# Triangles of all eight chunks issued together on four quarters of TensorE's array

## The chip, the cores and the metric

One core of a Trainium2 chip runs one program. TensorE (PE) multiplies matrices and writes to PSUM, of which it has eight banks; VectorE (DVE), ScalarE (ACT) and GpSimd (POOL) do elementwise work; transfers are issued from SyncE's queue (SP). The metric is the device time of one execution in microseconds. Three executions of the kernel before took 1361.43, 1364.46 and 1368.26 us.

## The reference

One layer over 256 latent tokens and 256 context tokens, each 2048 wide: a modulated norm, one wide input projection, two branches (RWKV-7 with 16 heads of 64, gated linear attention with 4 heads), two projections back, an output projection and a last norm. What matters here is the RWKV branch's scan, in both directions (`d`), context first, then latent:

```
def step(s, inp):
    w_t, k_t, v_t, a_t, b_t = inp[:5]
    sa = jnp.einsum("bhvk,bhk->bhv", s, a_t)
    s = s * w_t[:, :, None, :] + sa[..., None] * b_t[:, :, None, :] + v_t[..., None] * k_t[:, :, None, :]
    y = jnp.einsum("bhvk,bhk->bhv", s, inp[5]) if emit else None
```

## The kernel before

The scan is done in eight chunks of 64 tokens for each direction: four of context (`g` = 0) and four of latent tokens (`g` = 1). The 16 heads go in eight pairs `p`; a pair's two heads `hd` lie in the two halves of the 128 partitions. For each chunk the products of `a` and `b` inside it make a strictly triangular 64 x 64 matrix (a "triangle"), and the chunk's step needs the inverse of one minus it. The path of a pair:

- `fe_track` makes the factors `ar` (with decays, for `a` and `r`) and `bk` (for `b` and `k`).
- `ab_track` multiplies them to the triangles: 16 matmuls of 64 x 64 x 64 in fp32 for the context chunks into one PSUM bank (`pab`), an eviction with a mask into `AB` on DVE, and the same once more for the latent chunks. Head 0 uses the upper left quarter of the array (rows and columns 0 to 63), head 1 the lower right one.
- `gg_track` makes the value products, of which those of the first four chunks are `pgc`: 16 matmuls, with head 0 and head 1 in two row halves, both written to the same output half (`vs`), so into two banks.
- `inv_track` copies parts of `AB` to `Lin` and `GMo` (ACT), transposes `Lin` to `M` (DVE), and inverts the 32 x 32 triangles with 60 instructions on POOL (`tm`, `M`). Two transposes (`Lin<-M`), small matmuls (`pH`, `pZ`) and copies make the inverse `Z`.
- `sc_track` then runs the eight steps of the scan: `p1`, `R`, `pU`, `UV`, `pSs`, `Sn` and the output `pY`, on PE, ACT and DVE in turn.

All eight pairs' tracks are interleaved by a planner (`Issue`) when the program is built: it keeps a clock for each engine from rough costs, and issues the work that can start first, by priority. Between the small matmuls it places the dense stream (`acc`), the projections, whose weights are split into two parts `wH` (ACT) and `wL` (DVE) and multiplied three times. Each engine then runs its list in order. `pab`, `pgc` and the other small products share three banks (`g3`), claimed by the planner.

Of the kernel before, what the change touches and what calls it, by code (L numbers as in the profile page):

```python
# [12 lines left out]
OP = mybir.AluOpType  # L13
# [4 lines left out]
P = 128  # L18
# [58 lines left out]
class Issue:  # L77
# [136 lines left out]
    def rel(self, x):  # L214
        nm = x.tensor.name
        b = self.bank_of.pop(nm)
        self.busy.discard(b)
        self.bank_free[b] = self.rd.get(nm, 0.0)
# [112 lines left out]
def hybrid_layer(tc, a, out):  # L331
    nc = tc.nc
    es = ExitStack()
    with es:
# [6 lines left out]
        iss = Issue(ps, {"acc": (0, 1, 2, 3), "pa": (4, 5, 6, 7), "gg": (4, 5, 6, 7), "st": (2,), "u1": (3,), "py": (4,),  # L341
                         "g3": (5, 6, 7), "o2": (2, 3),
                         "f4": (0, 1, 2, 3, 4, 5, 6), "s1": (7,), "s2": (6, 7),
                         "xp": (0, 1, 2, 3, 4, 5, 6, 7)})
        rel = iss.rel
        engs = (nc.vector, "dve"), (nc.scalar, "act"), (nc.gpsimd, "pool"), (nc.tensor, "pe"), (nc.sync, "dma")
        V, S, G, T, Q = (Eng(iss, e, k, False) for e, k in engs)
        DV, AC, PO, PE, DM = (Eng(iss, e, k, True) for e, k in engs)
# [610 lines left out]
        def chunk(i, d):  # L959
            return i if d == 0 else (3 - i if i < 4 else 11 - i)  # L960
# [9 lines left out]
        def half(hd):  # L970
            return slice(64 * hd, 64 * hd + 64)
# [5 lines left out]
        RW = {}  # L977
# [127 lines left out]
        def ab_track(p, xp):  # L1105

            yield lambda: ("feat", p) in DONE and (p == 0 or ("lin", p - 1) in DONE)
            ar, bks = RW[p]["ar"], RW[p]["bks"]
            AB = RW["AB"]
            xb = p % 2  # L1110
            for g in range(2):
                pa = yield Claim("g3", [P, 4, 2, 64], "pab", *bks, ar)
                yield [PE.matmul(pa[half(hd), i, d, :], bks[d][half(hd), chunk(4 * g + i, d), xb, :], ar[half(hd), d, i, g, :],
                                 start=True, stop=True) for i in range(4) for d in range(2) for hd in range(2)]
                yield DV.tensor_tensor(AB[:, 4 * g:4 * g + 4], pa, RW["m_t"][:, None, None, :].to_broadcast([P, 4, 2, 64]), op=OP.mult)
                rel(pa)
            DONE.add(("ab", p))

        def gg_track(p, fp, xp):

            yield lambda: ("ab", p) in DONE
            s = RW[p]
            ar, bks = s["ar"], s["bks"]
            GM, GMr, BK = s["GM"], s["GMr"], s["BK"] = tuple(RW[n][p % 2] for n in ("GM", "GMr", "BK"))
            vs = rows(p)[1]
            xk = 1 - p % 2
            left = [6]

            def done():
                left[0] -= 1  # L1130
                if not left[0]:
                    DONE.add(("gg", p))

            def mask(m, n, r):
                return m[r, p % 2, None].to_broadcast([r.stop - r.start, n, 2, 64])

            def ev_c(pg, hd):
                yield DV.tensor_tensor(GM[vs, hd, 0:4], pg[vs], mask(m_ab, 4, vs), op=OP.mult)
                rel(pg)
                done()  # L1140

            def ev_l(pg, hd, i):
                yield DV.tensor_tensor(GM[vs, hd, 4 + i:6 + i], pg[vs, :, :, 0, :], mask(m_ab, 2, vs), op=OP.mult)
                yield DV.tensor_tensor(GMr[:, hd, i:i + 2], pg[:, :, :, 1, :], mask(m_r, 2, slice(0, P)), op=OP.mult)
                rel(pg)
                done()

            yield past(p, 3)
            pg = []
            for hd in range(2):  # L1150
                pg.append((yield Claim("g3", [P, 4, 2, 64], f"pgc{hd}", *bks, ar)))
            yield [PE.matmul(pg[hd][vs, i, d, :], bks[d][half(hd), chunk(i, d), xk, :], ar[half(hd), d, i, 0, :],
                             start=True, stop=True) for i in range(4) for d in range(2) for hd in range(2)]
            for hd in range(2):
                iss.spawn(3, ev_c(pg[hd], hd), "evc")
            iss.spawn(3, aq_track(p, xp), "aq")
            for i in (0, 2):
                yield past(p, 5 + i)
                pg = []
                for hd in range(2):  # L1160
                    pg.append((yield Claim("g3", [P, 2, 2, 2, 64], f"pgl{hd}", *bks, ar)))
                yield [PE.matmul(pg[hd][:, ii, d], bks[d][half(hd), chunk(4 + i + ii, d)].rearrange("p a b -> p (a b)"),
                                 ar[half(hd), d, i + ii, 1:3, :], start=True, stop=True)
                       for ii in range(2) for d in range(2) for hd in range(2)]
                for hd in range(2):
                    iss.spawn(3, ev_l(pg[hd], hd, i), "evl")

        def inv_track(p, fp, xp):

            yield lambda: ("ab", p) in DONE and (p < 2 or ("gi", p - 2) in DONE)
            s = RW[p]
            AB, Z = RW["AB"], RW["Z"][p % 2]
            h0 = 64 * (p % 2)
            hs = slice(h0, h0 + 64)
            qs = [slice(h0 + 32 * hd, h0 + 32 * hd + 32) for hd in range(2)]
            Lin, M, GMo = (RW[n][hs] for n in ("Lin", "M", "GMo"))
            for hd in range(2):  # L1180
                for blk in range(2):
                    r = slice(64 * hd + 32 * blk, 64 * hd + 32 * blk + 32)
                    cc = slice(32 * blk, 32 * blk + 32)
                    yield AC.copy(RW["Lin"][qs[hd]].rearrange("p t u -> p u t")[:, 16 * blk:16 * blk + 16, :],
                                  AB[r, :, :, cc].rearrange("p i d t -> p (i d) t"))
            yield DV.transpose(M.rearrange("p i c -> p (i c)"), Lin.rearrange("p t u -> p (t u)"))
            for hd in range(2):
                yield AC.copy(RW["GMo"][qs[hd]], AB[64 * hd:64 * hd + 32, :, :, 32:64].rearrange("p i d t -> p (i d) t"))
            DONE.add(("lin", p))
            yield lambda: p == 0 or ("sub", p - 1) in DONE  # L1190
            for j in range(1, 31):
                n = 31 - j
                tm = fp.tile([P, 256], F32, name="tm", tag="tm", bufs=1)
                tv = tm[hs, 0:n * j].rearrange("p (a b) -> p a b", b=j)
                yield PO.tensor_tensor(tv, M[:, j + 1:32, j:j + 1].to_broadcast([64, n, j]),
                                       M[:, j:j + 1, 0:j].to_broadcast([64, n, j]), op=OP.mult)
                yield PO.tensor_tensor(M[:, j + 1:32, 0:j], M[:, j + 1:32, 0:j], tv, op=OP.add)
            DONE.add(("sub", p))
            yield PO.memset(M.rearrange("p i c -> p (i c)")[:, ::33], 1.0)
            yield DV.transpose(Lin.rearrange("p u c -> p c u"), M.rearrange("p i c -> p c i"))  # L1200
            pH = yield Claim("g3", [P, 16, 32], "pH", Lin)
            hq = int(4)
            for u in range(0, 16, hq):
                yield [PE.matmul(pH[q, u + x, :], RW["GMo"][q, u + x, :], RW["Lin"][q, u + x, :], start=True, stop=True,
                                 tile_position=(q.start, q.start)) for x in range(hq) for q in qs]
            yield AC.copy(GMo, pH[hs])
            rel(pH)
            W = RW["Lin"].rearrange("p a b -> p (a b)").rearrange("p (i u) -> p u i", u=32)
            yield DV.transpose(W[hs].rearrange("p u i -> p i u"), M)
            pZ = yield Claim("g3", [P, 16, 32], "pZ", GMo, Lin)  # L1210
            for u in range(0, 16, hq):
                yield [PE.matmul(pZ[64 * hd:64 * hd + 32, u + x, :], RW["GMo"][qs[hd], u + x, :], W[qs[hd], 16 + u + x, :],
                                 start=True, stop=True, tile_position=(qs[hd].start, 64 * hd)) for x in range(hq) for hd in range(2)]
            yield lambda: p < 2 or ("sc1", p - 2) in DONE
            for hd in range(2):
                for blk in range(2):
                    r = slice(64 * hd + 32 * blk, 64 * hd + 32 * blk + 32)
                    yield (DV.tensor_copy if hd else AC.copy)(Z[r, :, 32 * blk:32 * blk + 32], W[qs[hd], 16 * blk:16 * blk + 16, :])
                yield (DV.tensor_copy if hd else AC.copy)(Z[64 * hd:64 * hd + 32, :, 32:64], pZ[64 * hd:64 * hd + 32])
            rel(pZ)  # L1220
            s["Z"] = Z
            DONE.add(("gi", p))
# [589 lines left out]
```

## Time and profile before

| | us |
|---|---|
| median of three runs | 1364.46 |
| profiled execution | 1361.36 |
| its span, first to last instruction | 1359.6 |
| PE busy | 1270.1 |
| DVE busy | 968.3 |
| ACT busy | 718.2 |
| POOL busy | 543.3 |

All recorded instructions have one line, L304, since one helper issues them; so groups are told apart by the names of their tiles. Matmuls on PE overlap: a matmul's time runs from its start to its modelled end, and starts can lie much closer than that. An fp32 matmul shows as two instructions.

### The profile page before, as it was taken

The page shows a single profiled execution, that of the slowest core. Times are in us where ns is not written, and L with a number is a line of the kernel's source. Part 1 is how long each engine was busy: PE and PEld are TensorE (multiplying, and loading weights), DVE is VectorE, ACT ScalarE, POOL GpSimd, SP SyncE. Part 2 cuts the span into 40 slices and gives each one's busy share as a digit, 9 for nine tenths or more (in the row PEclk, how much of TensorE's full clock was granted, in tenths as well). Part 3 has the DMA queues.
Part 4 walks back from the last instruction along what each step waited for, and adds up shares of the span by engine and source line. Part 5 has one row for each costly group of instructions (what it writes and reads, how often), then busy time and mean ns, then how long its engine had stood idle before and what let it go on. Part 6 is the DMA issues. An engine that isn't in the chain of part 4 may idle for free. (4 is left out here: it accounts for less than half of the span.)

```text
span 1359.6 us, 29662 instructions
## 1 busy us (share of the span) xinstructions
PE 1270.1 (93%) x11479; PEld 1068.1 (79%) x11479; DVE 968.3 (71%) x2031; ACT 718.2 (53%) x1449; POOL 543.3 (40%) x684
## 2 busy tenths in 40 slices
PE   5999999999999999999899999799989999999996
PEld 3555578688788897998777778677878888999876
DVE  4433497885965737767978998698978776668656
ACT  5222244343334444486577678667766666445443
POOL 0000476676570000005888729673983550000012
PEclk9999999999999999999889999799979999999999
DMA  9999465455462433576632443234433545789564
GB/s 347 354 340 311 132 195 168 150 171 160 145 202 79 134 102 97 153 196 171 157 85 76 113 118 92 77 99 114 108 78 94 138 105 145 203 247 271 185 230 144
DMA packets 311186, 220.45 MB, mean 162 GB/s; under 512 B 37354, under 2 KB 286724, under 8 KB 310532
## 3 DMA queue, kind: packets, MB, share of 16 engines
q1 hardware_dynamic: 311044, 218.55, 55.5%
q8 instruction: 90, 1.47, 0.4%
q14 instruction: 52, 0.43, 0.1%
HBM read 199.76 MB, written 12.46 MB: 156 GB/s over the span
## 5 line engine op out<-in xcount | busy, mean ns | idle before, releaser
L304 DVE TENSOR_TENSOR wL<-raw,wH 128x512 fp32r<-128x512 f32 x484 | 377.2, 786 | 170.2 <-ACT wH L304 165.0
L304 ACT CAST wH<-raw 128x512 fp32r<-128x512 f32 x484 | 295.1, 616 | 328.5 <-PE acc L304 208.7
L304 PE MATMUL acc<-lH,wH 128*128 128x256 f32 x896 | 285.1, 318 | 0.5 <-ACT tg L304 0.5
L304 PE MATMUL acc<-lL,wH 128*128 128x256 f32 x896 | 256.0, 286 | 0.0
L304 PE MATMUL acc<-lH,wL 128*128 128x256 f32 x896 | 255.6, 285 | 0.2 <-DVE wL L304 0.2
L304 PEld LDWEIGHTS acc<-lH,wH 128*128 128x128 f32 x896 | 173.4, 194 | 21.1 <-issue 4.5
L304 POOL TENSOR_TENSOR tm<-M 64x30 f32<-64x30 f32 (+14 forms) x240 | 160.1, 667 | 74.3 <-DVE M L304 48.1
L304 POOL TENSOR_TENSOR M<-M,tm 64x30 f32<-64x30 f32 (+14 forms) x240 | 170.1, 709 | 18.7
L304 PEld LDWEIGHTS acc<-lL,wH 128*128 128x128 f32 x896 | 174.5, 195 | 3.1 <-issue 1.7
L304 PEld LDWEIGHTS acc<-lH,wL 128*128 128x128 f32 x896 | 173.9, 194 | 0.4 <-DVE wL L304 0.4
L304 PE MATMUL acc<-hH,wH 128*128 128x512 f32 (+1 forms) x416 | 168.7, 406 | 1.3 <-ACT lo L304 1.3
L304 PE MATMUL acc<-hH,wL 128*128 128x512 f32 (+1 forms) x416 | 157.2, 378 | 0.0
L304 PE MATMUL acc<-hL,wH 128*128 128x512 f32 (+1 forms) x416 | 156.3, 376 | 0.1
L304 PEld LDWEIGHTS acc<-hH,wH 128*128 128x128 f32 x416 | 78.6, 189 | 38.1 <-issue 22.9
L304 POOL TENSOR_TENSOR xs<-yg,fg 128x512 f32<-128x512 f32 (+1 forms) x10 | 13.5, 1371 | 231.4 <-DVE yg L304 231.4
L304 POOL TENSOR_TENSOR gw<-gw,csl 128x512 f32<-128x512 f32 x60 | 71.1, 1185 | 61.9 <-DMA gw<-in_w_mod_dram 61.9
L304 PEld LDWEIGHTS acc<-hH,wL 128*128 128x128 f32 x416 | 78.4, 188 | 15.5 <-DVE wL L304 0.4
L304 POOL TENSOR_TENSOR ga<-ga,gw 128x512 f32<-128x512 f32 x60 | 88.6, 1476 | 4.2
L304 PEld LDWEIGHTS acc<-hL,wH 128*128 128x128 f32 x416 | 78.9, 190 | 10.6 <-DVE hL L304 0.4
L304 PE MATMUL acc<-yH,wH 128*128 128x256 f32 x256 | 73.0, 285 | 0.0
L304 PE MATMUL acc<-yL,wH 128*128 128x256 f32 x256 | 72.8, 284 | 0.0
L304 PE MATMUL acc<-yH,wL 128*128 128x256 f32 x256 | 72.8, 284 | 0.0
(318 smaller groups left out, 2627.7 us busy)
## 6 DMA issues: line engine op xcount, KB each, us to landing
raw<-in_w_in_dram SPq DMA_DIRECT2D x174, 512.0 KB, 4.0
wm<-in_w_mod_dram SPq DMA_DIRECT2D x64, 512.0 KB, 6.9
gw<-in_w_mod_dram SPq DMA_DIRECT2D x64, 256.0 KB, 4.0
raw<-in_w_out_dram SPq DMA_DIRECT2D x32, 512.0 KB, 4.8
raw<-in_w_b_dram SPq DMA_DIRECT2D x16, 512.0 KB, 4.1
raw<-in_w_a_dram SPq DMA_DIRECT2D x16, 512.0 KB, 4.9
kv<-kvo SPq DMA_DIRECT2D x16, 256.0 KB, 3.9
tg<-tg SPq DMA_DIRECT2D x32, 128.0 KB, 3.8
```

The source lines that it names most:

```text
L304: op = Op("dma" if name == "dma_start" else self.key, name, lambda: f(*a, **k), aps[0], aps[1:], func, k.get("accum_out"), any(x.tensor.na ...
```

## The change

The triangles of both groups of chunks are issued in one list, for `g` = 0 and 1 in turn, into two banks claimed together. For `g` = 1 the heads' output halves are exchanged (`hd ^ g`), so that the four matmuls of a chunk number and direction use all four quarters of the array. `Lin` and `GMo` are therefore copied for each `g` apart, in twice as many copies of half the size. The value products `pgc` go to one bank, each head into its own output half; their evictions read from there.

On PE, at the first pair's triangles, stood in the kernel before:

```order
L304 MATMUL acc<-lH,wL 128x256
L304 MATMUL pab<-ar,bk 64x64 x16
L304 MATMUL acc<-lH,wH 128x256
L304 MATMUL acc<-lL,wH 128x256
L304 MATMUL acc<-lH,wL 128x256
L304 MATMUL pab<-ar,bk 64x64 x16
L304 MATMUL acc<-lH,wH 128x256
```

And there stand now (the two numbers of `bk` are the directions, `pab0` and `pab1` the two groups of chunks):

```order
L304 MATMUL acc_6537<-lH_1431,wL_6547 128x256
L304 MATMUL pab0_6638<-ar_6073,bk_6429 64x64 x2
L304 MATMUL pab1_6639<-ar_6073,bk_6429 64x64 x2
L304 MATMUL pab0_6638<-ar_6073,bk_6531 64x64 x2
L304 MATMUL pab1_6639<-ar_6073,bk_6531 64x64 x2
```

These four rows come four times, and only then the next dense matmul: the second burst has moved up to the first.

On DVE, at the second pair, whose `AB` evictions meet the transposes `Lin<-M` of the first pair's inverse, stood before:

```order
L304 TENSOR_TENSOR AB<-pab,m_t 128x512
L304 TENSOR_TENSOR wL<-raw,wH 128x512
L304 STREAM_TRANSPOSE Lin<-M 64x32x32
L304 TENSOR_TENSOR AB<-pab,m_t 128x512
L304 TENSOR_TENSOR bv<-pb,vc 128x256
L304 STREAM_TRANSPOSE Lin<-M 64x1024
L304 STREAM_TRANSPOSE M<-Lin 64x1024
```

And there stand now:

```order
L304 STREAM_TRANSPOSE Lin<-M 64x32x32
L304 TENSOR_TENSOR AB<-pab_7372,m_t 128x512
L304 TENSOR_TENSOR AB<-pab_7373,m_t 128x512
L304 TENSOR_TENSOR bv<-pb,vc 128x256
L304 TENSOR_TENSOR wL<-raw,wH 128x512
L304 STREAM_TRANSPOSE Lin<-M 64x1024
L304 STREAM_TRANSPOSE M<-Lin 64x1024
```

Both evictions are now behind the first transpose; before it was the second alone.

On ACT, at the same pair, `Lin` and the copy `GMo<-pH` of the pair before stood so:

```order
L304 COPY Lin<-AB 32x16x32 x2
L304 COPY GMo<-pH 64x512
L304 COPY Lin<-AB 32x16x32 x2
L304 ACTIVATE sq<-kc,vec 128x512
L304 COPY GMo<-AB 32x512 x2
```

And now:

```order
L304 COPY Lin<-AB 32x8x32 x5
L304 COPY GMo<-pH 64x512
L304 COPY Lin<-AB 32x8x32 x3
L304 CAST wH<-raw 128x512
L304 COPY GMo<-AB 32x256 x4
```

Five short copies instead of two long ones now stand ahead of `GMo<-pH`. Since the planner decides everywhere, the order differs from the first triangles to the end.

```diff
@@ ab_track
+            pas = []
             for g in range(2):
-                pa = yield Claim("g3", [P, 4, 2, 64], "pab", *bks, ar)
-                yield [PE.matmul(pa[half(hd), i, d, :], bks[d][half(hd), chunk(4 * g + i, d), xb, :], ar[half(hd), d, i, g, :],
-                                 start=True, stop=True) for i in range(4) for d in range(2) for hd in range(2)]
-                yield DV.tensor_tensor(AB[:, 4 * g:4 * g + 4], pa, RW["m_t"][:, None, None, :].to_broadcast([P, 4, 2, 64]), op=OP.mult)
-                rel(pa)
+                pas.append((yield Claim("g3", [P, 4, 2, 64], f"pab{g}", *bks, ar)))
+
+            yield [PE.matmul(pas[g][half(hd ^ g), i, d, :], bks[d][half(hd), chunk(4 * g + i, d), xb, :], ar[half(hd), d, i, g, :],
+                             start=True, stop=True) for i in range(4) for d in range(2) for g in range(2) for hd in range(2)]
+            for g in range(2):
+                yield DV.tensor_tensor(AB[:, 4 * g:4 * g + 4], pas[g], RW["m_t"][:, None, None, :].to_broadcast([P, 4, 2, 64]),
+                                       op=OP.mult)
+                rel(pas[g])
@@ gg_track
             def ev_c(pg, hd):
-                yield DV.tensor_tensor(GM[vs, hd, 0:4], pg[vs], mask(m_ab, 4, vs), op=OP.mult)
-                rel(pg)
+                h = half(hd)
+                yield DV.tensor_tensor(GM[vs, hd, 0:4], pg[h], m_ab[h, 1 - hd, None].to_broadcast([64, 4, 2, 64]), op=OP.mult)
...
-            pg = []
-            for hd in range(2):
-                pg.append((yield Claim("g3", [P, 4, 2, 64], f"pgc{hd}", *bks, ar)))
-            yield [PE.matmul(pg[hd][vs, i, d, :], bks[d][half(hd), chunk(i, d), xk, :], ar[half(hd), d, i, 0, :],
+            pg = yield Claim("g3", [P, 4, 2, 64], "pgc", *bks, ar)
+            yield [PE.matmul(pg[half(hd), i, d, :], bks[d][half(hd), chunk(i, d), xk, :], ar[half(hd), d, i, 0, :],
@@ inv_track
             for hd in range(2):
-                for blk in range(2):
-                    r = slice(64 * hd + 32 * blk, 64 * hd + 32 * blk + 32)
-                    cc = slice(32 * blk, 32 * blk + 32)
-                    yield AC.copy(RW["Lin"][qs[hd]].rearrange("p t u -> p u t")[:, 16 * blk:16 * blk + 16, :],
-                                  AB[r, :, :, cc].rearrange("p i d t -> p (i d) t"))
+                for g in range(2):
+                    for blk in range(2):
+                        r = slice(64 * (hd ^ g) + 32 * blk, 64 * (hd ^ g) + 32 * blk + 32)
+                        cc = slice(32 * blk, 32 * blk + 32)
+                        yield AC.copy(RW["Lin"][qs[hd]].rearrange("p t u -> p u t")[:, 16 * blk + 8 * g:16 * blk + 8 * g + 8, :],
+                                      AB[r, 4 * g:4 * g + 4, :, cc].rearrange("p i d t -> p (i d) t"))
...
             for hd in range(2):
-                yield AC.copy(RW["GMo"][qs[hd]], AB[64 * hd:64 * hd + 32, :, :, 32:64].rearrange("p i d t -> p (i d) t"))
+                for g in range(2):
+                    yield AC.copy(RW["GMo"][qs[hd], 8 * g:8 * g + 8, :],
+                                  AB[64 * (hd ^ g):64 * (hd ^ g) + 32, 4 * g:4 * g + 4, :, 32:64].rearrange("p i d t -> p (i d) t"))
```

## Rows read from the trace of the kernel before

**Rows 1.** The page: busy time by engine, and PE's clock in 40 slices.
```profile
PE 1270.1 (93%) x11479; PEld 1068.1 (79%) x11479; DVE 968.3 (71%) x2031; ACT 718.2 (53%) x1449; POOL 543.3 (40%) x684
PEclk9999999999999999999889999799979999999999
```
**Rows 2.** Busy us (instructions) PE, PEld, DVE, ACT, POOL; clock, DMA share, GB/s.
```profile
616.20:1166.30 550.10, 506.79 (x6338) 436.93 (x6337) 447.45 (x951) 374.59 (x796) 346.91 (x509) 0.95 0.43 111
```
**Rows 3.** By window, tile `M` alone: length, DVE busy, POOL busy, clock, DMA.
```profile
625.60:674.10 48.50, 0.00 (x0) 43.88 (x61) 0.93 0.57 150
683.10:734.10 51.00, 1.24 (x1) 43.84 (x61) 0.92 0.33 90
...
1065.00:1107.50 42.50, 0.00 (x0) 37.86 (x61) 1.00 0.56 143
sum 372.50, DVE 9.04 POOL 329.99; mean DVE 1.13 POOL 41.25
```
**Rows 4.** Waits from 600 to 1157 us: us in total, times, longest.
```profile
POOL tm L304 <- DVE M L304: 48.1, 5, 30.8
```
**Rows 5.** Timeline around a late inverse, DVE then PE: start, us, engine, what.
```profile
857.68 2.03 DVE L304 STREAM_TRANSPOSE Lin<-M 64x1024 f32<-64x1024 f32 x1 [5.61 <-POOL M L304]
860.47 0.68 DVE L304 TENSOR_TENSOR AB<-pab,m_t 128x512 f32<-128x512 f32 x1
859.76 1.06 PE L304 MATMUL pH<-Lin,GMo 32*32 32x32 f32 x32 [6.89 <-DVE Lin L304]
```
**Rows 6.** Timeline of PE at the first pair's triangles and value products.
```profile
616.01 0.28 PE L304 MATMUL acc<-lH,wL 128*128 128x256 f32 x1
616.22 1.15 PE L304 MATMUL pab<-ar,bk 64*64 64x64 f32 x32
617.30 0.39 PE L304 MATMUL acc<-lH,wH 128*128 128x256 f32 x1
617.52 0.28 PE L304 MATMUL acc<-lL,wH 128*128 128x256 f32 x1
...
617.85 1.15 PE L304 MATMUL pab<-ar,bk 64*64 64x64 f32 x32
...
619.91 1.15 PE L304 MATMUL pgc<-ar,bk 64*64 64x64 f32 x32
```
**Rows 7.** Timeline of PE at other places where small matmuls run side by side.
```profile
24.20 0.64 PE L304 MATMUL pg<-wm,cs 128*32 128x256 f32 x8 [0.28 <-DVE modv L304]
...
722.59 1.10 PE L304 MATMUL pab<-ar,bk 64*64 64x64 f32 x31
723.62 0.39 PE L304 MATMUL acc<-lH,wH 128*128 128x256 f32 x1
...
724.28 0.22 PE L304 MATMUL pU<-R,Z 64*64 64x64 f32 x2
724.31 0.22 PE L304 MATMUL pgc<-ar,bk 64*64 64x64 f32 x1
724.34 0.22 PE L304 MATMUL pU<-R,Z 64*64 64x64 f32 x2
```
**Rows 8.** ACT's copies by shape, 600 to 1157 us: busy, mean ns, idle before.
```profile
L304 ACT COPY Lin<-AB 32x512 f32<-32x512 f32 x32 | 34.8, 1088 | 19.0 <-DVE AB L304 18.6
L304 ACT COPY UV<-pV 64x256 f32<-64x256 f32 x56 | 18.8, 366 | 1.6 <-PE pV L304 1.0
L304 ACT COPY R<-p 128x128 f32<-128x128 f32 x64 | 16.5, 258 | 13.0 <-PE p L304 12.2
L304 ACT COPY GMo<-AB 32x512 f32<-32x512 f32 x16 | 9.8, 614 | 0.2
```
**Rows 9.** Timeline at the seventh pair, ACT then PE, and the window behind it.
```profile
982.39 4.45 ACT L304 COPY Lin<-AB 32x512 f32<-32x512 f32 x4 [0.72 <-DVE AB L304]
988.89 2.37 PE L304 MATMUL pgl<-ar,bk 64*128 64x128 f32 x16 [2.42 <-ACT rs L304]
988.80:1002.30 13.50, 13.41 (x144) 11.85 (x144) 9.17 (x16) 7.30 (x16) 11.54 (x27) 0.50 0.16 42
```

More of the change, by code (lines that the diff above doesn't have):

```diff
@@ L1126, in gg_track @@
             xk = 1 - p % 2
-            left = [6]
+            left = [6, 2]
             def done():
@@ L1137, in ev_c @@
             def ev_c(pg, hd):
-                yield DV.tensor_tensor(GM[vs, hd, 0:4], pg[vs], mask(m_ab, 4, vs), op=OP.mult)
-                rel(pg)
+                h = half(hd)
+                yield DV.tensor_tensor(GM[vs, hd, 0:4], pg[h], m_ab[h, 1 - hd, None].to_broadcast([64, 4, 2, 64]), op=OP.mult)
+                left[1] -= 1
+                if not left[1]:
+                    rel(pg)
                 done()
@@ L1148, in gg_track @@
             yield past(p, 3)
-            pg = []
-            for hd in range(2):
-                pg.append((yield Claim("g3", [P, 4, 2, 64], f"pgc{hd}", *bks, ar)))
-            yield [PE.matmul(pg[hd][vs, i, d, :], bks[d][half(hd), chunk(i, d), xk, :], ar[half(hd), d, i, 0, :],
+            pg = yield Claim("g3", [P, 4, 2, 64], "pgc", *bks, ar)
+            yield [PE.matmul(pg[half(hd), i, d, :], bks[d][half(hd), chunk(i, d), xk, :], ar[half(hd), d, i, 0, :],
                              start=True, stop=True) for i in range(4) for d in range(2) for hd in range(2)]
             for hd in range(2):
-                iss.spawn(3, ev_c(pg[hd], hd), "evc")
+                iss.spawn(3, ev_c(pg, hd), "evc")
             iss.spawn(3, aq_track(p, xp), "aq")
```

## Prediction

> **What bounds the kernel now.** I read the head of the page first: TensorE (PE) is busy for 1270 of 1359.6 us, and its clock row stands at 9 tenths or more nearly everywhere [rows 1]. Then the table by stretch: the change sits between the first `pab` burst at 616.2 us and the last scan's end at 1166.3 us. Of these 550.1 us PE is busy for 506.8, so 43.3 us are plain idle time, and the granted clock averages 0.95; GpSimd (POOL) is busy for 346.9 [rows 2]. From 0.05 of 550 us, some 55 us ran at half clock, 1.2 GHz instead of 2.4. So PE is nearly full, but not full.
>
> Then the view by window of POOL on tile `M`: the triangular inverse of a head pair takes 42.5 to 51.5 us, eight of them 372.5 us [rows 3]. They run from 625.6 to 1107.5, 481.9 us, so POOL stands between inverses for 481.9 - 372.5 = 109.4 us. A pair's inverse can start only after its `pab` matmuls, the two `AB` evictions on VectorE (DVE), the `Lin` copies on ScalarE (ACT) and a transpose on DVE; the waits say so (POOL waits for DVE's `M` for 48.1 us in 5 places) [rows 4]. This chain and PE's stock of work run neck and neck: where the chain is late PE stands still, as before the `pH` at 859.76, for 6.89 us; there DVE was held at the transpose `Lin<-M` for 5.61 us by POOL, and the second `AB` eviction of the next pair, queued behind it, ran only at 860.47 [rows 5].
>
> **PE's part of the change.** In a burst of 32 `pab` instructions (two for each fp32 matmul) between dense matmuls, the dense start before it is at 616.01 and the next at 617.30; without the burst these lie 0.12 apart, and the first dense step behind it is 0.22 long instead of 0.12 [rows 6]. So a burst costs 1.29 - 0.12 + 0.10 = 1.27 us. Six of the eight second bursts stand beside small matmuls of the scan instead, where one costs what it holds: 723.62 - 722.59 = 1.03 for 31 instructions [rows 7]. The two instructions of a step run side by side: 16 steps in 1.15 - 0.22 = 0.93 us, 0.058 each.
>
> The changed order has all 64 instructions together, on all four quarters. If four run in a step as two do now, the joint burst costs what one costs, and the second is gone: 2 x 1.27 + 6 x 1.05 = 8.8 us over the eight pairs. The trace has no burst on all four quarters, so this has bounds. At worst pairs follow each other, 32 steps of 0.058: then only the switch goes, 1.27 - 0.93 = 0.34 at two places and 0.1 to 0.2 at six, about 1.5 us. At best it is 8.8 and some half-clock time. I take 8.8, by the nearest rows: `pgc`, whose two row halves write the same output half, takes 1.15 as `pab` does on the diagonal [rows 6]; two `pU` and one `pgc`, on three quarters, start within 0.03 us, and the next step comes 0.06 later [rows 7]; four column strips of `pg` run together, 8 instructions of 256 columns in 0.64 us, two steps [rows 7].
>
> The Trainium skill speaks against this in "TensorE: Matmul & The Clock Gate", section "Seeing it yourself" ("Wait — 56ns, not 53.3ns?"): starts never come closer than about 25 ns. By it 64 starts take an estimated 1.6 us and PE saves 3.4 us instead of 8.8. The trace disagrees for matmuls on different quarters: three starts lie within 0.03 us.
>
> **The `pgc` matmuls** keep their number and go from two banks in one output half to one bank on the diagonal. That is the place of `pab` before, and both take 1.15 [rows 6]: nothing. The skill's "TensorEngine Tiling (Array Packing)", "Gotcha 1: PSUM Pressure", says that different row tiles cannot use one PSUM bank at a time; by that the eight bursts would take 0.93 more each, 7.4 us. The `pab` rows disagree: two row halves in one bank at 0.058 a step. The evictions on DVE keep their number and sizes, and cost nothing new. Two of three banks of the pool are now claimed at once for `pab`, and one instead of two for `pgc`; I put these against each other.
>
> **ACT's part.** `Lin` goes from 32 copies to 64 of half the size, `GMo` from 16 to 32. The fixed cost of a copy follows from two lengths: 366 ns for 256 elements and 258 for 128 make 0.84 an element and 150 ns fixed [rows 8]. So half a `Lin` copy takes 150 + (1088 - 150)/2 = 620 ns, and half a `GMo` 150 + (614 - 150)/2 = 382. That adds 32 x 0.15 + 16 x 0.15 = 7.2 us to ACT, which is busy for 374.6 of the 550 us [rows 2]; bounds: nothing, if a copy's time goes by its length alone, and 48 x 0.258 = 12.4, if each added copy costs as much as that short one. Of it `GMo` (0.3 a pair) lies beside the inverse, hidden; `Lin` (0.6 a pair) is on the inverse's chain, and behind it in ACT's queue wait the scan's `R` and `UV` copies and the dense stream's `wH`.
>
> **The chain.** At the first pair the second burst ends at 617.85 + 1.15 = 619.00 [rows 6], and with an eviction of 0.68 [rows 5] `AB` is there 3.5 us after the start; a joint burst and two evictions are 2.6. So 0.9 less a pair, and 0.6 more for `Lin`: 0.3 x 8 = 2.4 us where it decides. But the order moves too. Before, the `pab` of pairs 1, 2, 4 and 6 (from 0) stood ahead of the `pH` of the pair before; now only those of 1, 3, 5 and 7 do. The handover 0 to 1 cost 9.0 us (674.1 to 683.1) [rows 3]; now both `AB` evictions stand behind `Lin<-M` there, so 2.0 + 2 x 0.68 + 8 x 0.62 + 0.6 + 1.2 = 10. Adding up the gaps between inverses in the new order by such sums: 10 (0 to 1), 14, about 0 (2 to 3), 36, about 0 (4 to 5), 21, 10 (6 to 7), together some 91 instead of 109. (The 14 are two transposes, `pH`, and then `pab` to `M`; the 36 hold some 23 us of PE work between `pH` and the next `pab`, the 21 some 9, counted in the new order, dense matmuls at 0.12 and small ones at their measured pitch.) The work behind the last `pH` up to the scan's end, counted alike, grows from 52 us to 57. That is -13. Where pairs now follow without a gap, PE's own work (about 97 us a double) and half clocks would hold the second `pH` back by some 3 each, twice: -7. PE's own sum, -8.8, and the chain's, -7, lie close.
>
> **Sum.** -7.2 us, since neither path can gain more than the other lets it. Against the profiled execution's own 1361.36 us (span 1359.6 and 1.8 around it) that is 1354.2; the median of the runs shown, 1364.46, is 3.1 higher, so 1357. All of this lies in the middle stretch: what comes behind the last scan is dense work and loads, which the change doesn't touch. A change of less than 0.5% (6.8 us: under 1357.6 or over 1371.3 counts) can't be told from none here.
>
> **Rivals.**
> - Both paths gain fully: the order leaves fewer standstills and with them fewer half-clock stretches (55 us of these cost up to 27 now). PE's 8.8 and 5 of clock: 14, 1350.5. For it: `pab` bursts, short of work, stand near several clock drops. Against: the idle time comes from POOL's lateness, which stays.
> - The inverse paces everything: PE arrives at `pH` 1 us earlier and waits 1 us longer; with the gaps rearranged but not shorter, -1 to -3, 1362.5. For it: the waits for `pH` [rows 5]. Against: PE is busy 92% of the stretch.
> - The array doesn't go four wide: PE saves 1.5, ACT's `Lin` costs about 2 on the chain: 1365. Against it: rows 7. The skill's bank rule, if it held, would add 7.4 to this; I give that 1 in 100.
> - Slower: the eight `Lin` copies block ACT's queue. Already now four of them, 4.45 us from 982.39, hold the `rs` activations back until PE has stood 2.42 us before `pgl`, and then the clock is at half for 13.5 us [rows 9]. With 0.9 us more on ACT for each pair (7.2) and two more such half-clock stretches (13.5 x 0.5 = 6.7 each), against 8.8 saved: +11.8, 1376. It decides if PE then stands over 2 us at `pgl`, `pq` or a scan step in two more pairs than now. For it: four of the eight trains now stand among the scan's copies in ACT's order. Against: a train as a whole is only 0.6 longer.
>
> **From this to numbers.** The forecast has 0.44 (its own range 1352 to 1362), full gain 0.19, absorbed 0.14, not four wide 0.06, slower 0.17. The forecast lies on the bound of 1357.6, so half of it counts as faster: 0.22 + 0.19 + 0.01 = 0.42; slower is the last rival and a little of the fourth case, 0.17; the same 0.41. For 8 in 10 I leave out the lower half of full gain and most of the slow case: 1347 to 1371.
>
> **What would show it.** `pab` as 64 instructions in about 1.1 us, starts in fours, 0.058 apart; `pab` holding PE for 8.6 us in all instead of 17; 64 `Lin` copies of 0.62 and 32 `GMo` of 0.38; POOL's inverses spanning about 470 us instead of 482; PE idle time in the stretch near 43 us. I am wrong if `pab` takes 2 us, if the idle time grows by what PE saved, if half `Lin` copies cost far from 0.62, or if half-clock time moves by over 10 us.

## The result: 1.5% slower

The changed kernel takes 1384.3 us (median of four; 1383.4 to 1388.3) beside 1362.95 for the kernel before: a ratio of 1.0152, 95% interval 1.0121 to 1.0183. The forecast was 1357, the range 1347 to 1371; the slow rival stood at 1376 with a chance of 0.17.

The profiled execution (1383.83 us, span 1382.1 instead of 1359.6) has lost 19.9 of its 22.5 us in the middle stretch, from the first `pab` to the last `pyt`; the stretch also begins 3.3 us later. The table by window, busy us of PE, PEld, DVE, ACT and POOL, then clock, DMA share and GB/s, beside [rows 2]:

```profile
619.50:1189.50 570.00, 512.14 (x6350) 440.10 (x6349) 459.13 (x952) 383.97 (x845) 336.95 (x509) 0.93 0.42 108
```

570.0 us instead of 550.1. PE stands idle for 57.9 us instead of 43.3, and the clock averages 0.93 instead of 0.95. If PE runs at 1.2 instead of 2.4 GHz for the missing part, that is some 80 us at half clock against 55, and costs up to 12 us. And PE holds less for `pab`; this is the first pair's burst, to be set against [rows 6]:

```profile
619.30 0.28 PE L304 MATMUL acc<-lH,wL 128*128 128x256 f32 x1
619.51 1.16 PE L304 MATMUL pab<-ar,bk 64*64 64x64 f32 x64
620.60 0.39 PE L304 MATMUL acc<-lH,wH 128*128 128x256 f32 x1
```

64 instructions in the time of 32: the array does run four wide. Eight bursts at 1.09, as from 619.51 to 620.60, instead of sixteen at 1.08 make 8.6 us less. Idle time, clock and bursts together, 14.6 + 12 - 8.6 = 18, come near the 19.9 us; the clock has only two digits, so this is rough.

The longest wait of PE is at the seventh pair. The timelines of ACT and PE:

```profile
1010.51 5.03 ACT L304 COPY Lin<-AB 32x256 f32<-32x256 f32 x8 [2.15 <-DVE AB L304]
1015.57 0.59 ACT L304 ACTIVATE SD<-Sn,Dt 128x64 f32<-128x64 f32 x2
1016.06 0.39 ACT L304 COPY GMo<-AB 32x256 f32<-32x256 f32 x1
1016.35 0.25 ACT L304 COPY R<-p 128x128 f32<-128x128 f32 x1
```

```profile
1010.28 0.28 PE L304 MATMUL acc<-lH,wL 128*128 128x256 f32 x1
1016.66 0.69 PE L304 MATMUL pU<-R,Z 64*64 64x64 f32 x8 [6.09 <-ACT R L304]
1017.14 1.92 PE L304 MATMUL pgc<-ar,bk 64*64 64x64 f32 x32
```

The scan needs `R`, a copy of 0.25 us; it stands in ACT's list behind the train of eight `Lin` copies, which in turn waits for `AB`. PE stands for 6.09 us, from 1010.57 on. The clock is at half from about 1012.2, within that wait, until 1022.3 (`pgc` takes 1.92 us there instead of 1.15):

```profile
1012.20:1022.30 10.10, 5.64 (x65) 5.19 (x66) 4.42 (x9) 7.08 (x17) 4.55 (x12) 0.50 0.41 100
```

The same happens at the third pair, where `pq` waits for `BK`, some way behind the train in ACT's list, and at the fourth, fifth and sixth, where `pSs` waits for ACT's `UV`:

```profile
756.15 2.07 PE L304 MATMUL pq<-sq,bo 128*128 128x512 f32 x2 [5.07 <-ACT BK L304]
...
807.51 0.69 PE L304 MATMUL pSs<-UV,BK 128*64 128x64 f32 x8 [3.04 <-ACT UV L304]
...
892.29 0.45 PE L304 MATMUL pSs<-UV,BK 128*64 128x64 f32 x8 [2.39 <-ACT UV L304]
...
942.30 0.45 PE L304 MATMUL pSs<-UV,BK 128*64 128x64 f32 x8 [2.04 <-ACT UV L304]
```

The inverses on POOL, beside [rows 3]; the gaps between them lie between one row's end and the next one's start:

```profile
628.70:678.40 49.70, 0.00 (x0) 43.59 (x61) 0.93 0.56 143
688.20:736.80 48.60, 0.00 (x0) 43.97 (x61) 0.90 0.35 91
751.40:803.10 51.70, 0.00 (x0) 38.53 (x61) 0.97 0.37 94
808.60:848.20 39.60, 3.32 (x2) 34.98 (x61) 0.84 0.39 91
894.20:941.90 47.70, 0.00 (x0) 40.86 (x61) 0.94 0.38 99
943.40:988.50 45.10, 3.29 (x2) 40.47 (x61) 0.92 0.36 85
1016.90:1060.50 43.60, 0.00 (x0) 38.97 (x61) 0.94 0.34 89
1076.10:1119.40 43.30, 0.00 (x0) 38.67 (x61) 0.92 0.48 128
sum 369.30, DVE 6.61 POOL 320.05; mean DVE 0.83 POOL 40.01
```

From the first start at 628.7 to 1119.4 they take 490.7 us, 121.4 of them gaps; forecast were 91.

That is not the whole loss. The stretch behind the last inverse, up to the end of the scan, in the kernel before and now:

```profile
1107.50:1166.30 58.80, 58.39 (x736) 51.39 (x734) 40.50 (x108) 35.29 (x90) 0.09 (x1) 1.00 0.49 131
1119.40:1189.50 70.10, 68.96 (x827) 60.21 (x826) 42.11 (x117) 38.31 (x99) 0.07 (x1) 0.90 0.43 117
```

So 11.3 of the 19.9 us lie behind the last inverse. PE hardly waits there in either kernel, but now it has 827 instructions left instead of 736, and the clock is at 0.90 instead of 1.00.

### The profile page after: what moved, and what is told of

Its sections match the earlier page's. It is cut to its first block, busy times and chain, and to the rows that moved or that the text cites. A ratio compares the mean times of both kernels' runs of the same rounds, so it can differ in the third digit from the quotient of the medians.

```text
span 1382.1 us, 29706 instructions
## 1 busy us (share of the span) xinstructions
PE 1276.7 (92%) x11479; PEld 1071.2 (78%) x11479; DVE 977.4 (71%) x2031; ACT 726.7 (53%) x1497; POOL 531.4 (38%) x684
## 4 chain that ended last, share of the span: by engine, by line
PE 60%; DVE 18%; POOL 7%; ACT 6%; issue 4%; DMA 4%; SPq 0%; DVEq 0%; ACTq 0%
PE acc L304 35%; PE pv L304 6%; DVE wL L304 5%; PE pout L304 4%; POOL tm L304 3%; POOL M L304 3%; ACT Lin L304 3%; PE pg L304 3%; PE pS L304 1%; PE p L304 1%; DMA raw<-in_w_out_dram 1%; DVE kvo L304 1%; PE pSs L304 1%; PE pU L304 1%; PE pY L304 1%
## 5 line engine op out<-in xcount | busy, mean ns | idle before, releaser
L304 POOL TENSOR_TENSOR M<-M,tm 64x30 f32<-64x30 f32 (+14 forms) x240 | 160.4, 668 | 18.8
L304 POOL TENSOR_TENSOR ga<-ga,gw 128x512 f32<-128x512 f32 x60 | 85.6, 1427 | 4.2
```

The source lines that it names most:

```text
L304: op = Op("dma" if name == "dma_start" else self.key, name, lambda: f(*a, **k), aps[0], aps[1:], func, k.get("accum_out"), any(x.tensor.na ...
```

## Experiments

Two theories stood at the start. "Order": the instructions are as good as before, but the planner's new order of them is worse. "Work": the 48 more copies on ACT cost the time. Three kernels take order and work apart, by letting the planner reckon with one form of an instruction and issuing another; every engine keeps its list. All ratios are to the kernel before, run beside the kernel in question.

**The new order with the old work.** The changed kernel's order, two quarters, long copies (an excerpt; `GMo` likewise):

```diff
@@ ab_track: planned on four quarters, issued on two
+    plan = PE.matmul(pas[g][half(hd ^ g), i, d, :], a_, b_, start=True, stop=True)
+    real = PE.matmul(pas[g][half(hd), i, d, :], a_, b_, start=True, stop=True)
+    plan.call = real.call
...
@@ inv_track: of two planned half copies the first issues one long copy, the second nothing
+    plan.call = (lambda: None) if g else AC.copy(dst[:, 16 * blk:16 * blk + 16, :],
+                                                 AB[r, :, :, cc].rearrange("p i d t -> p (i d) t")).call
```

> The changed kernel's order on every engine, with the work of the kernel before in it: both bursts of triangles together but on two quarters (head 0 upper left, head 1 lower right, 0.058 us a pair), and 4 long Lin and 2 long GMo copies per pair of heads instead of 8 and 4 short ones. Theory 'order' (the new order sets trains of Lin copies among the scan's copies on ACT, PE then waits for the scan and falls to half clock): 1380 to 1392, that is as slow as the changed kernel or slower by what four quarters saved, 7.5 us, less what short copies cost. Theory 'work' (the extra copies on ACT cost the time): 1362 to 1370.

1379.1 us, ratio 1.0123 (1.0086 to 1.0159), just under the range for "order" and far from that for "work". With the triangles and copies of the kernel before in it, the new order is 17 us slower than the kernel before, and 2 to 5 us faster than the changed kernel. Only `pgc` stays in one bank; a run further down shows that its matmuls take the same time there. The same place, with four long copies in the train (4.22 us from 1007.41):

```profile
1012.96 0.69 PE L304 MATMUL pU<-R,Z 64*64 64x64 f32 x8 [5.44 <-ACT R L304]
```

**The new order, short copies, two quarters.**

The matmuls are those of the run before; the short copies stay, and read what these write:

```diff
+    r = slice(64 * hd + 32 * blk, 64 * hd + 32 * blk + 32)
+    plan.call = AC.copy(dst[:, 16 * blk + 8 * g:16 * blk + 8 * g + 8, :],
+                        AB[r, 4 * g:4 * g + 4, :, cc].rearrange("p i d t -> p (i d) t")).call
```

> The changed kernel's order and its short copies, but triangles on two quarters. Theory 'order' and theory 'work' alike: what four quarters are worth in this order. PE holds pab 16 x 0.058 = 0.93 us longer for each of 8 pairs, 7.5 us; if PE paces, 1390 to 1393; if PE's savings vanish in waits, 1384 to 1387.

1378.1 us, ratio 1.0122 (1.0082 to 1.0161): below both ranges, and not slower than the changed kernel, though its bursts take 2.08 us instead of 1.16. So the run was made once more beside the changed kernel:

> The changed kernel unchanged, once more, beside the next run on the same chip. Theory 'order': 1380 to 1388 as before, PE idle about 58 us in the stretch and half-clock time near 85 us again if four quarters cost clock, near 60 if the 85 was chance.

> The changed kernel's order with its triangles on two quarters, once more. If four quarters cost clock in this order: 4 to 7 us faster than the run beside it. If they save what PE holds less: 3 to 7 us slower. If PE's saving vanishes in waits: within 2 us.

1381.3 with four quarters, 1379.5 with two; ratios 1.0143 (1.0117 to 1.0169) and 1.0128 (1.0102 to 1.0153). PE holds `pab` for 8 us longer on two quarters and the time is the same within the intervals. The stretches, four quarters first:

```profile
616.40:1187.90 571.50, 510.46 (x6364) 439.19 (x6363) 461.46 (x952) 384.16 (x845) 340.24 (x509) 0.93 0.40 108
```

```profile
617.50:1183.20 565.70, 508.64 (x6364) 439.69 (x6363) 463.38 (x952) 382.30 (x845) 341.37 (x509) 0.95 0.41 109
```

On four quarters PE idles for 61.0 us, on two for 57.1, and the clock is at 0.93 against 0.95, in both pairs of profiles. That is some 80 us at half clock against 57. The seventh pair shows how the saving is lost; its burst and the `pU` behind it, four quarters first:

```profile
1004.04 1.16 PE L304 MATMUL pab<-ar,bk 64*64 64x64 f32 x64
...
1014.58 0.69 PE L304 MATMUL pU<-R,Z 64*64 64x64 f32 x8 [6.09 <-ACT R L304]
```

```profile
1003.15 2.08 PE L304 MATMUL pab<-ar,bk 64*64 64x64 f32 x64
...
1013.68 0.69 PE L304 MATMUL pU<-R,Z 64*64 64x64 f32 x8 [5.15 <-ACT R L304]
```

The burst is 0.92 us shorter on four quarters, the wait for `R` is 0.94 longer, and `pU` starts 10.54 us behind the burst's start instead of 10.53. DVE comes to the eviction of the burst into `AB` no sooner, and ACT's train follows that eviction: these two set the pace here. In this order what PE saves comes back as waiting and as half clock.

**The old order with the short copies.**

```diff
+    two = [AC.copy(RW["Lin"][qs[hd]].rearrange("p t u -> p u t")[:, 16 * blk + 8 * g:16 * blk + 8 * g + 8, :],
+                   AB[r, 4 * g:4 * g + 4, :, cc].rearrange("p i d t -> p (i d) t")) for g in range(2)]
+    plan.call = lambda two=two: [x.call() for x in two]
```

> The kernel before, its order held, with each long Lin and GMo copy issued as two short ones (64 and 32 copies, 0.62 and 0.38 us, 7.2 us more on ACT). Theory 'order': 1363 to 1368, at most a third of 7.2 us on the path. Theory 'work': 1375 or more.

1359.5 us, ratio 0.9978 (0.9953 to 1.0003), below both ranges. The groups of ACT show the copies a little dearer than forecast (620 and 382 ns):

```profile
L304 ACT COPY Lin<-AB 32x256 f32<-32x256 f32 x64 | 35.8, 640 | 15.5 <-DVE AB L304 15.1
L304 ACT COPY GMo<-AB 32x256 f32<-32x256 f32 x32 | 11.3, 399 | 0.2
```

So 48 more copies cost nothing in the old order. "Work" has fallen.

**One part of the change at a time,** each with the order the planner gives it. First the joint bursts and the short copies, in the kernel before (an excerpt of the change's diff):

```diff
-    pa = yield Claim("g3", [P, 4, 2, 64], "pab", *bks, ar)
+    pas.append((yield Claim("g3", [P, 4, 2, 64], f"pab{g}", *bks, ar)))
...
+    yield [PE.matmul(pas[g][half(hd ^ g), i, d, :], bks[d][half(hd), chunk(4 * g + i, d), xb, :], ar[half(hd), d, i, g, :],
+                     start=True, stop=True) for i in range(4) for d in range(2) for g in range(2) for hd in range(2)]
```

> Only the triangles' part of the change (one burst on four quarters, short copies); the value products as before in two banks. Its own order. Theory 'order' names no size in advance for a new order: what counts is how many Lin trains stand among the scan's R and UV copies on ACT. With PE stalls of over 2 us behind them as in the changed kernel: 1375 to 1390; without: 1355 to 1365. Rival 'the joint burst itself is at fault': 1380 or more whatever the stalls.

1380.0, ratio 1.0128 (1.0100 to 1.0156). That fits "order", and it lies on the bound of the rival, so this run alone doesn't part them. Its two longest waits, 5.3 and 5.1 us, are of `pq` for ACT. This one stands behind a train of seven `Lin` copies in ACT's list (4.53 us from 933.42):

```profile
941.82 2.07 PE L304 MATMUL pq<-sq,bo 128*128 128x512 f32 x2 [5.27 <-ACT sq L304]
```

Then `pgc` in one bank, alone (an excerpt):

```diff
-    pg.append((yield Claim("g3", [P, 4, 2, 64], f"pgc{hd}", *bks, ar)))
+    pg = yield Claim("g3", [P, 4, 2, 64], "pgc", *bks, ar)
...
```

> Only the value products' part (both heads in one bank on the diagonal); triangles in two bursts and long copies as before. Its own order. If two row halves could not write one bank at once, pgc would take 2.1 us instead of 1.1 in each of 8 pairs. Theory 'order': pgc stays at 1.1, and any change of time comes with stalls elsewhere; 1355 to 1385.

1383.3, ratio 1.0158 (1.0129 to 1.0186), without a single joint burst or short copy. The `pgc` matmuls themselves are unchanged in one bank (median 218 ns, PE 10.1 us in all, before 10.3). Its longest stall is at another place and of another kind, `pSs` behind DVE:

```profile
863.86 0.58 PE L304 MATMUL pSs<-UV,BK 128*64 128x64 f32 x5 [6.32 <-DVE UV L304]
```

Against the rival: a joint burst isn't needed for the loss. Each of two parts with nothing in common costs about as much as both together. That made a third theory: the order of before is a good draw, that is, a lucky one of the many orders that the planner could make, and any change draws anew.

**Neutral draws.** Two numbers of the planner changed, the program's work not at all:

```diff
-                win = 40
+                win = 30
```

> The kernel before; only the planner's window, within which it goes by priority and not by time, is 30 instead of 40. The same instructions in another order. Theory 'good draw' (the order of before is a good one among many, and a new one costs time whatever made it): 1368 to 1385. Rival 'this change's orders are bad' (trains of Lin copies among the scan's, brought by the new bursts): 1355 to 1368.

1382.1, ratio 1.0104 (1.0071 to 1.0137). The stretch, and its longest stall:

```profile
619.30:1180.00 560.70, 508.41 (x6303) 437.49 (x6303) 454.45 (x947) 370.91 (x791) 352.10 (x509) 0.94 0.41 107
```

```profile
999.04 0.70 PE L304 MATMUL p<-UV,GM 128*64 128x64 f32 x8 [5.49 <-DVE UV L304]
```

```diff
-    LAT = {"pe": 200.0, "act": 135.0, "dve": 135.0, "pool": 135.0, "dma": 920.0}
+    LAT = {"pe": 200.0, "act": 145.0, "dve": 135.0, "pool": 135.0, "dma": 920.0}
```

> The kernel before; only the planner's latency behind an ACT instruction is 145 instead of 135. As in the run ahead of this: theory 'good draw' 1368 to 1385, rival 'this change's orders are bad' 1355 to 1368.

1378.9, ratio 1.0088 (1.0056 to 1.0119). The same in the changed kernel:

> The changed kernel; only the planner's latency behind an ACT instruction is 145 instead of 135. Theory 'good draw': its time moves by several us either way from 1383, within 1365 to 1390, though no instruction differs. Rival 'the change's instructions or its joint claim cost the time': 1380 to 1388.

1373.1, ratio 1.0051 (1.0030 to 1.0071): about 13 us faster than the changed kernel by the ratios, through a number that means nothing. Both neutral draws of the kernel before lost, 12 and 14 us by their ratios. So an order alone moves this kernel by 12 to 14 us, and the old order is the best of the three drawn with the old costs for the kernel before.

**True costs in the planner.** It counts a `Lin` half copy at 307 ns (94 + 0.833 x 256), which takes 629:

```diff
-            c = (51 if psum else 94) + 0.833 * n + 93 * per
+            wide = any(s >= 32 and k > 1 for x in [out, *ins] for s, k in x.ap[-1:])
+            c = 150 + 1.83 * n if wide and name == "copy" else (51 if psum else 94) + 0.833 * n + 93 * per
```

> The changed kernel, but the planner counts copies with a step of 32 elements (Lin and Z) at what the trace shows, 150 ns and 1.83 ns an element, instead of 94 ns and 0.83; the order follows from that. Theory 'order': the trains move out of the scan's way or the scan is planned around them, PE's stalls behind Lin trains (1.2 + 3.0, 2.4, 2.0, 6.1 us) shrink: 1355 to 1374. Theory 'work': 1380 or more.

1366.7, ratio 1.0029 (1.0008 to 1.0051). The scan's copies now stand inside the train instead of behind it, as here at the fourth pair:

```profile
809.06 0.61 ACT L305 COPY Lin<-AB 32x256 f32<-32x256 f32 x1
809.70 0.27 ACT L305 COPY R<-p 128x128 f32<-128x128 f32 x1
809.99 1.25 ACT L305 COPY Lin<-AB 32x256 f32<-32x256 f32 x2
811.05 0.29 ACT L305 COPY UV<-pU 64x128 f32<-64x128 f32 x1
811.37 2.55 ACT L305 COPY Lin<-AB 32x256 f32<-32x256 f32 x4
```

PE's wait for `R` at that place is 3.4 us, its longest for ACT now; in the changed kernel the longest was 6.1. But PE's waits as a whole are hardly fewer: it idles for 55.3 us in the stretch, instead of 57.9, and waits 16.6 us for `Lin` before `pH`, where the changed kernel waited 2.5:

```profile
616.10:1195.60 579.50, 524.18 (x6553) 454.53 (x6552) 472.89 (x977) 391.01 (x861) 356.46 (x509) 0.94 0.43 115
```

```profile
PE pH L305 <- DVE Lin L305: 16.6, 6, 7.5
```

So that the moved trains gained the 17 us is not shown; more dense work now lies inside the stretch, and what comes behind it is 169.9 us long instead of 192.6.

> The kernel before with the planner counting strided ACT copies at their measured cost, as in the changed kernel's run with true costs (1366.7). Theory 'good draw': 1364 to 1380, since a better cost makes up for the lost draw only in part. Rival: below 1362.

1365.2, ratio 0.9998 (0.9976 to 1.0020). By the ratios the changed kernel with true costs is 4 us above the kernel before, and the kernel before with true costs level with it.

The last four runs ask what four quarters are worth in such an order, and whether a further draw does better. The first two are the changed kernel with true costs, on four quarters and, by the exchange shown above, on two:

> The changed kernel with true costs in the planner, once more, as the partner of the next run: 1364 to 1370.

> The same order with its triangles on two quarters instead of four. If PE's saving of 7.5 us counts in a good order: 4 to 8 us slower than the run beside it. If it is lost in waits and half clock as in the changed kernel's own order: within 2 us, or faster.

1367.5, ratio 1.0039 (1.0018 to 1.0060), and 1370.3, ratio 1.0056 (1.0037 to 1.0076): 2.8 us for four quarters, of 8 that PE holds less. That is between the two expectations, and the intervals overlap, so this is unclear.

The other two change the window or the latency in it, as above:

> The changed kernel with true costs and the planner's window at 30: another draw. By the spread of draws so far (1373 to 1384 with the old costs, 1365 to 1367 with true ones) 1360 to 1375.

> The changed kernel with true costs and the planner's ACT latency at 145: another draw, 1360 to 1375. Under 1358 it would beat the kernel before.

1376.9, ratio 1.0095 (1.0066 to 1.0124), just over the expected range, and 1371.1, ratio 1.0057 (1.0034 to 1.0079). True costs don't end the scatter either. No run beat the kernel before beyond its interval.

Over all orders that the planner drew by itself, the changed kernel has ratios of 1.003 to 1.015, and the kernel before, with its neutral draws and true costs, of 1.000 to 1.010. These ranges overlap, so whether the change gains or loses by itself is not shown.

## Why the prediction was wrong

- **PE's term** was right as a mechanism and a size: 8.8 us forecast, 8.6 by the first pair's bursts. The sentence of the Trainium skill ("TensorE: Matmul & The Clock Gate", "Wait — 56ns, not 53.3ns?") that starts never come closer than about 25 ns, which stands there for back-to-back matmuls, doesn't carry over to different quarters: 64 starts lie within 0.95 us (1.16 less the last one's 0.22), 15 ns apart on average. But in the new order the time saved was not gained: two quarters were as fast.
- **`pgc`**: its matmuls cost nothing more, as forecast. The Trainium skill ("TensorEngine Tiling (Array Packing)", "Gotcha 1: PSUM Pressure") says that different row tiles cannot use one PSUM bank at a time; this is not borne out for matmuls on the diagonal (10.1 us in one bank, 10.3 in two). But "nothing" for the whole part, and "I put these against each other" for the claims of banks, failed: the part alone, in the order that came with it, took 21 us longer.
- **ACT's term** was right: 64 x 0.629 - 32 x 1.088 + 32 x 0.402 - 16 x 0.614 = 8.5 us more, 7.2 forecast. In the old order it is off the path.
- **The step that failed** is the chain's, which was to gain 7 us: "Adding up the gaps between inverses in the new order by such sums ... some 91 instead of 109". The gaps came to 121.4 us, and the inverses span 490.7 us instead of the forecast 470. The handover 0 to 1 was met (9.8, forecast 10), 1 to 2 too (14.6, 14), but 2 to 3 took 5.5 instead of 0, 3 to 4 took 46.0 instead of 36, 5 to 6 took 28.4 instead of 21, 6 to 7 took 15.6 instead of 10. The work behind the last `pH` was to grow by 5 us; what lies behind the last inverse grew by 11.3, with the clock at 0.90. The sums took each chain at its bare length, with 6 us in all for PE's own work and half clocks. The new order's waits behind ACT's queue and its 25 us more at half clock are not in them. Which wait lengthened which gap was not taken apart. Nor do the gaps alone set the time: in the kernel before with true costs they come to some 130 us by its trace, and the time is level with the old one.
- **The same error lies in the sum.** "Neither path can gain more than the other lets it", with an idle time "near 43 us", took that idle time as the kernel's, when it belonged to one order. Six other orders, drawn with the old costs (the changed kernel and its neutral draw, its two parts alone, the two neutral draws of the kernel before), idled for 52 to 61 us in the stretch and took some 7 to 21 us longer by their ratios. Idle time in the stretch doesn't explain every order, though: the changed kernel with true costs idles for 55.3 us there and is only 4 us slower.
- **Two of its own signs of being wrong came true:** the idle time grew by more than PE saved (14.6 us, 8.6 saved), and the time at half clock by some 25 us, where 10 was the bound.
- **The slow rival** had the place right (`Lin` trains in ACT's queue ahead of the scan's copies, then half clock), and its condition was met: PE stands over 2 us behind such trains at five pairs, in the kernel before at two (2.96 and 2.42 us). It got too little chance, and its price, 12, was low by 8. The argument against it, "a train as a whole is only 0.6 longer", counted the wrong thing: what matters is what stands behind the train, and that is the order's. That it explains the loss alone is not shown: `pgc` in one bank alone lost as much, and the neutral draws 12 and 14 us, with their longest waits elsewhere.

Left open: which property of the old order makes it good. With true costs the changed kernel got back some 17 of 21 us, but the two further draws with them lie 4 and 10 us above the first, and a neutral draw with the old costs lies between these two. So that the costs did it, and not the luck of a draw, is not shown.

## What to carry to other kernels

Where a planner sets the order, a change of a few microseconds in one place is measured against the scatter of orders; so measure that first, by changing a number of the planner that means nothing. To learn what an edit's instructions are worth, hold the order and exchange them in place. And look in the trace for trains of copies in a queue that runs in order, where they hold back a short one on which TensorE waits; a planner that counts them too cheap doesn't see this. Correcting such a cost is reasonable, but these runs don't show by themselves that it pays.

## What was not expected of the hardware

In the changed kernel's order, four quarters ran at a lower clock than two. The profiles on four show 0.93 in the stretch and those on two 0.95, twice each. Over the whole of every execution the granted clock was 0.963 to 0.972 in ten on four quarters (median 0.965), and 0.965 to 0.977 in ten on two (median 0.972). The time is the same though PE holds 8 us less.

In the true-cost order this doesn't come again: the stretch shows 0.94 and 0.93 in two profiles on four quarters and 0.94 on two, and the median over whole executions is 0.970 on four (22) and 0.967 on two (7). So it is not shown that four quarters as such cost clock. At the seventh pair, shown above, PE had stood for 1.6 of its 6.09 us when the clock fell. Whether the packed bursts themselves add falls was not tested apart.
